# Turning the softmaxed tiles of nine attention pairs with VectorE and DRAM instead of TensorE

## The chip, the cores and the metric

The kernel runs on one core of a Trainium2 chip. The metric is the device time of one execution in microseconds (us); before the change it is 1721.01 us, the median of three runs that lie between 1719.12 and 1723.49 us. The core has a matrix engine (TensorE, PE), a vector engine (VectorE, DVE), a scalar engine (ScalarE, ACT), a general engine (GpSimd, POOL) and a queue engine that only issues transfers (SyncE, SP). Each of them works through its own list of instructions in order and waits for the others by semaphores. ACT and POOL issue transfers too, in the same list as their computation.

## The reference, cut to what matters

One layer of a hybrid backbone on 512 latent tokens of width 1024 (and 256 context tokens) is computed: a modulated norm, one input projection, three mixers side by side, an output projection, and an expert feed-forward part. The change lies in the third mixer, a neighbourhood attention with eight heads of width 64. The tokens are a grid of 8 rows by 64 columns; each query sees a window of 16 columns in all rows, and all 256 context tokens:

```python
s_loc = jnp.einsum('bqhd,bkwhd->bhqkw', q_row, k_blk).astype(jnp.float32) + bias[None]
s_ctx = jnp.einsum('bqhd,bchd->bhqc', q_row, k_ctx).astype(jnp.float32)
s_all = jnp.concatenate([s_loc.reshape(b, h, GRID_W, kh * GRID_W), s_ctx], axis=-1)
p = jax.nn.softmax(s_all, axis=-1).astype(v.dtype)
p_loc = p[..., :kh * GRID_W].reshape(b, h, GRID_W, kh, GRID_W)
return (jnp.einsum('bhqkw,bkwhd->bqhd', p_loc, v_blk)
        + jnp.einsum('bhqc,bchd->bqhd', p[..., kh * GRID_W:], v_ctx))
```

The product of `p` and the values sums over keys, so TensorE needs `p` with keys on the partitions, while the softmax leaves it with queries on the partitions. Each tile of `p` therefore has to be transposed between the two.

## The kernel before, in words

The queries are cut into four groups of 128 (16 columns in all 8 rows). With eight heads this makes 32 units, and two heads that lie together in one tile make a pair: 16 pairs, called 0 to 15 here. A unit has one tile of 128 queries by 512 keys (256 of the window's rows, 256 of the context). The work on it goes through small functions:

- `a_scores(m)` (L1166): eight matmuls of PE write the scores of both heads of pair m into two tiles `sps` in PSUM. There are only two such tiles, so the scores of the next pair wait until the exponentials of this pair have read them.
- `a_min(n)` (L1175, L1176): DVE takes the minimum over a row and adds the bias `nb`.
- `a_exp(n)` (L1183): ACT's exponential, from PSUM into the tile `pr`.
- `a_norm(n)` (L1188, L1189): DVE's reciprocal of the row sum; then the scaling of `pr`, by DVE for the pair's first head and by POOL for its second.
- `a_T(n)` (L1196): four PE transposes of 128 by 128 into PSUM; `a_copy(n)` (L1201): ACT's copy into the SBUF tile `pT`.
- `a_values(m)` (L1214): sixteen matmuls of PE into the PSUM tile `po`; `a_out(m)` (L210, L213): ACT rounds `po` to the high part `mBh`, DVE subtracts for the low part `mBl`.

Around this stands the output projection. A table of steps (`plan`, filled by `at(step, function, arguments)`) sets the order on all engines by hand. Pair m owns four steps from `a0 = A0 + 4 * m`. In these steps PE also works on 20 groups of six matmuls of the output projection (`o_part`, L220 to L222), one to two a pair; ACT and DVE convert the weights they need (`i_high` and `i_low`: `wh` at L210 and `wl` at L213, 128 by 1024); SP loads weights into four buffers `wraw` (L241), ACT loads the bias tiles `nb` (L1106). The values of pair m - 2 are computed with the scores of pair m. After the last pair, PE goes on with the rest of the output projection, and some of it is already drawn in between the last pairs.

Of the kernel before, what the change touches and what calls it, by code (L numbers as in the profile page):

```python
# [7 lines left out]
F32 = mybir.dt.float32  # L8
# [4 lines left out]
AF = mybir.ActivationFunctionType  # L13
# [4 lines left out]
P = 128  # L18
# [7 lines left out]
NH = 16  # L26
# [131 lines left out]
def build(tc, A, out, dbg=None):  # L158
    nc = tc.nc
    V, S, G, PE = nc.vector, nc.scalar, nc.gpsimd, nc.tensor  # L160
# [131 lines left out]
    gs_d = tc.dram_tile([P, NU], F32, name="gs_d")  # L292
    rs_d = tc.dram_tile([P, NU], F32, name="rs_d")
    mod_d = tc.dram_tile([2, 4, 512], F32, name="mod_d")
    cs_d = tc.dram_tile([2, NX * NH, P], F32, name="cs_d")

    def rstd_of(pool, ssq, n, width):
# [60 lines left out]
    for t in range(NT):  # L358
        src = A["x"][t * P:(t + 1) * P, :] if t < NX else A["ctx"][(t - NX) * P:(t - NX + 1) * P, :]
# [61 lines left out]
    def a_copy(e):  # L421
        am[e] = a1.tile([P, 256], F32, name="mod0", bufs=2)
        S.activation(am[e], aps[:, e % 2 * 256:e % 2 * 256 + 256], AF.Copy)
# [68 lines left out]
    for t in range(1, NT):  # L492
# [7 lines left out]
        if t < 4:  # L500
            x_copy(t - 1, 1)
    x_copy(3, 1, True)
    a_copy(0)
    w_split(0)
    x_copy(4, 1, True)
# [5 lines left out]
    for step in START:  # L511
        {"u": u_high, "l": u_low, "w": w_split, "v": w_low, "f": a_mod, "c": a_copy, "x": x_copy, "g": g, "a": a_mm, "gh": gh, "gl": gl}[step[0]](*step[1:])
# [150 lines left out]
    for cb in range(12):  # L663
# [5 lines left out]
        n = SEQ  # L669
        if cb < 10:  # L670
            S.activation(xp[:, 515:771], pc[:, :CTX], AF.Copy)
            n = 770
# [10 lines left out]
        dst = xsn[:, :, cb * P:(cb + 1) * P] if cb < 8 else Bn[:, :, (cb - 8) * P:(cb - 7) * P]  # L683
# [120 lines left out]
    def at(step, f, *a):  # L804
        plan.setdefault(step, []).append((f, a))
# [249 lines left out]
    for c in range(4):  # L1055
        b = U0 + UP * c
# [11 lines left out]
    for c in range(4):  # L1068
        b = O1 + OP * c
# [30 lines left out]
    au, pos_ = {}, {}  # L1100
# [48 lines left out]
    nat = natp.sb("na3", bufs=4)  # L1149
# [42 lines left out]
    def a_T(n):  # L1192
# [3 lines left out]
            PE.transpose(pt[:, j, :], pr[:, j * P:(j + 1) * P], ident)  # L1196
        au[n] = pt

    def a_copy(n):
        pT = nat.tile([P, 4, P], F32, name="pT")  # L1200
        S.activation(pT, au[n], AF.Copy)  # L1201
        au[n] = pT

    def a_values(m):

        hp, g, _ = units[2 * m]
        vl = vls[g]
        po = pos_[0] = psP.tile([P, P], F32, name="po")
        pTs = [au.pop(2 * m + hh) for hh in range(2)]
        for j in range(4):  # L1210
            for hh in range(2):
                h = hp * 2 + hh
                vv = vl[:, j, h * 64:(h + 1) * 64] if j < 2 else vc[:, j - 2, h * 64:(h + 1) * 64]
                PE.matmul(po[64 * hh:64 * hh + 64, :], vv, pTs[hh][:, j, :], start=j == 0, stop=j == 3)  # L1214

    def a_out(n):
        hp, g, _ = units[2 * n]
# [3 lines left out]
    for m in range(16):  # L1221
        a0 = A0 + 4 * m
        for hh in range(2):
            at(a0 + 2 + 2 * hh, a_load, 2 * m + 4 + hh)
        if m < 4:
            at(a0, v_load, m)
        at(a0, a_scores, m)
        if m:
            at(a0, a_T, 2 * m - 2)
            at(a0, a_copy, 2 * m - 2)  # L1230
        if m > 1:
            at(a0, a_values, m - 2)
            at(a0 + 1, a_out, m - 2)
        for hh in range(2):
            at(a0 + hh, a_min, 2 * m + hh)
            at(a0 + hh + 1, a_exp, 2 * m + hh)
            at(a0 + hh + 2, a_norm, 2 * m + hh)
        if m:
            at(a0 + 2, a_T, 2 * m - 1)
            at(a0 + 2, a_copy, 2 * m - 1)  # L1240
    a0 = A0 + 64
    at(a0, a_T, 30)
    at(a0, a_copy, 30)
    at(a0, a_values, 14)
    at(a0 + 1, a_out, 14)
    at(a0 + 2, a_T, 31)
    at(a0 + 2, a_copy, 31)
    at(a0 + 5, a_values, 15)
    at(a0 + 6, a_out, 15)


    wop = Pools()
# [3 lines left out]
    h = o1.tile([P, NX, D], F32, name="h")  # L1256
# [965 lines left out]
```

## Time and profile before

| | |
|---|---|
| median of three runs | 1721.01 us (1719.12 to 1723.49) |
| the profiled execution | 1722.26 us, span 1720.5 us |
| PE busy | 1698.8 us (99% of the span) |
| DVE busy | 1406.3 us (82%) |
| ACT busy | 839.4 us (49%) |
| POOL busy | 385.8 us (22%) |
| granted TensorE clock | 0.997 of full speed over the span |
| first scores of pair 0 | 361.14 us after the span's start |
| last values of pair 15 | 455.2 us after the span's start |

The time of the profiled execution is 1.76 us longer than the span, which begins with the first recorded instruction and ends with the last. Busy matmuls are pipelined, and a matmul that stands in the queue behind another counts as busy while it waits for its operand, so 99% is not the share in which PE computes. Attention takes some 95 us of 1720. How the engines share a stretch of the span is read from a view that sums busy time between two moments; what an engine waited for is read from the list of instructions in order of time, where the time in brackets is the idle time before the instruction and the name behind the arrow what ended it.

### The profile page before, as it was taken

Reading aid. Unit: us, or ns where it says so; the run is one execution under the profiler, and the core shown is the slowest. Engines: PE = TensorE matmul, PEld = TensorE weight load, DVE = VectorE, ACT = ScalarE, POOL = GpSimd, SP = SyncE. Lnnn points to the kernel's source line nnn. Section 1 sums busy time; section 2 is a strip of 40 time slices with the busy share of each in tenths; the row PEclk is TensorE's granted clock in tenths of the full one; section 3 lists DMA queues with packets and bytes.
Section 4 is the critical chain, followed back from the end, with each engine's and each line's share of the span. In section 5 each row is a group of like instructions: output and inputs, shape, how many; then the busy total and the mean of one; then the engine's idle time right before and its main releaser. Section 6 shows DMA issues by size and latency. Waiting matters only on the chain.

```text
span 1720.5 us, 26491 instructions
## 1 busy us (share of the span) xinstructions
PE 1698.8 (99%) x9556; PEld 1473.3 (86%) x9556; DVE 1406.3 (82%) x2668; ACT 839.4 (49%) x1507; POOL 385.8 (22%) x307
## 2 busy tenths in 40 slices
PE   9999999999999999999999999999999999999997
PEld 7888776776789889999999998888888888888886
DVE  6689479976546699879989997998988989889886
ACT  5443355565534333656776774444444444444444
POOL 0003134012336444031212111212211212211200
PEclk9999999999999999999999999999999999999999
DMA  9457466485536334587999999999999999999972
GB/s 368 134 158 233 153 201 176 147 277 164 167 107 196 115 117 135 173 290 266 349 348 348 342 328 353 386 404 365 392 364 380 368 418 382 385 366 381 383 275 106
DMA packets 200068, 473.08 MB, mean 275 GB/s; under 512 B 15080, under 2 KB 119112, under 8 KB 181984
## 3 DMA queue, kind: packets, MB, share of 16 engines
q1 hardware_dynamic: 151584, 268.41, 45.7%
q0 software_dynamic: 21136, 144.83, 22.0%
q10 hardware_dynamic: 27216, 58.14, 9.1%
q8 instruction: 75, 1.23, 0.3%
q14 instruction: 57, 0.47, 0.1%
HBM read 418.17 MB, written 55.26 MB: 275 GB/s over the span
## 4 chain that ended last, share of the span: by engine, by line
PE 82%; DVE 8%; DMA 3%; ACT 3%; issue 2%; ACTq 0%; SPq 0%; POOL 0%; DVEq 0%; POOLq 0%
PE pv L222 10%; PE pv L221 10%; PE pv L220 10%; PE pu L220 8%; PE pu L222 8%; PE pu L221 8%; PE acc L220 5%; PE acc L221 5%; PE acc L222 5%; DMA act_d<-act 3%; DVE wl L213 2%; PE acc L459 1%; PE acc L464 1%; PE acc L461 1%; PE sps L1166 1%
## 5 line engine op out<-in xcount | busy, mean ns | idle before, releaser
L210 ACT ACTIVATE wh<-wraw 128x1024 fp32r<-128x1024 f32 x328 | 342.0, 1053 | 219.3 <-PE acc L221 75.5
L213 DVE TENSOR_TENSOR wl<-wraw,wh 128x1024 fp32r<-128x1024 f32 x295 | 360.5, 1233 | 87.1 <-ACT wh L210 86.4
L220 PE MATMUL pu<-u2h,wh 128*128 128x368 f32 x1008 | 336.8, 334 | 1.5 <-ACT act L1516 1.3
L222 PE MATMUL pu<-u2h,wl 128*128 128x368 f32 x1008 | 332.3, 330 | 2.2 <-DVE wl L213 2.2
L221 PE MATMUL pu<-u2l,wh 128*128 128x368 f32 x1008 | 331.8, 329 | 0.0
L222 PE MATMUL pv<-wh,wwl 128*128 128x512 f32 x768 | 299.3, 390 | 0.0
L221 PE MATMUL pv<-wl,wwh 128*128 128x512 f32 x768 | 299.1, 389 | 0.0
L220 PE MATMUL pv<-wh,wwh 128*128 128x512 f32 x768 | 299.0, 389 | 0.1
L1795 POOL DMA_INDIRECT row<-in_peer_uv,idxG x128 | 158.3, 1236 | 615.7 <-DVE accG L1809 568.0
L222 PEld LDWEIGHTS pu<-u2h,wl 128*128 128x128 f32 x1008 | 189.6, 188 | 3.6 <-DVE wl L213 3.4
L220 PEld LDWEIGHTS pu<-u2h,wh 128*128 128x128 f32 x1008 | 189.7, 188 | 3.2 <-ACT act L1516 1.8
L221 PEld LDWEIGHTS pu<-u2l,wh 128*128 128x128 f32 x1008 | 189.8, 188 | 1.4
L210 ACT ACTIVATE wwh<-gd 128x384 fp32r<-128x384 f32 x124 | 65.1, 525 | 242.6 <-DVE gd L2040 229.8
L222 PEld LDWEIGHTS pv<-wh,wwl 128*128 128x128 f32 x768 | 144.2, 188 | 30.4 <-DVE wwl L213 0.3
L220 PEld LDWEIGHTS pv<-wh,wwh 128*128 128x128 f32 x768 | 144.2, 188 | 29.3 <-ACT wwh L210 0.5
L221 PEld LDWEIGHTS pv<-wl,wwh 128*128 128x128 f32 x768 | 144.1, 188 | 29.1
L1809 DVE SCALAR_TENSOR_TENSOR accG<-row,wG,accG 128x1024 f32<-128x1024 f32 x127 | 162.4, 1279 | 1.6
L1800 DVE CUSTOM_DVE_ANT_0 row<-row,u2G 128x1024 f32<-128x1024 f32 x128 | 154.8, 1218 | 0.0
L1883 ACT ACTIVATE stg<-gdps 128x512 f32<-128x512 f32 x96 | 100.9, 1163 | 19.5 <-ACT act L1516 14.9
L213 POOL TENSOR_TENSOR wl<-wraw,wh 128x1024 fp32r<-128x1024 f32 x33 | 79.1, 2402 | 101.7 <-ACT wh L210 71.2
L1516 ACT ACTIVATE act<-pu 128x368 f32<-128x368 f32 x90 | 42.7, 475 | 105.6 <-PE pu L222 61.5
L213 DVE TENSOR_TENSOR wwl<-gd,wwh 128x384 fp32r<-128x384 f32 x124 | 69.0, 556 | 21.9 <-ACT wwh L210 21.9
(481 smaller groups left out, 3017.3 us busy)
## 6 DMA issues: line engine op xcount, KB each, us to landing
wraw<-in_peer_ut SPq DMA_DIRECT2D x128, 512.0 KB
wraw<-in_peer_uv SPq DMA_DIRECT2D x128, 512.0 KB
gd<-gd_d SPq DMA_DIRECT2D x15, 1536.0 KB
gd_d<-stg ACTq DMA_DIRECT2D x11, 2048.0 KB
wraw<-in_w_in SPq DMA_DIRECT2D x40, 512.0 KB
acl<-act_d SPq DMA_DIRECT2D x92, 184.0 KB
act_d<-act ACTq DMA_DIRECT2D x90, 184.0 KB
cs<-cs_d SPq DMA_DIRECT2D x32, 256.0 KB
```

Of the source, the lines that this page charges most:

```text
L210: S.activation(hi, full, AF.Copy)
L213: (eng or V).tensor_tensor(lo, full, hi.bitcast(F32), ALU.subtract)
L220: PE.matmul(ps, ah, bh, start=start, stop=False)
L221: PE.matmul(ps, ah, bl, start=False, stop=False)
L222: PE.matmul(ps, al, bh, start=False, stop=stop)
L459: PE.matmul(px, h[:, k, :], uh[:, k, :], start=s, stop=False)
L461: PE.matmul(px, h[:, k, :], ul[:, k, :], start=False, stop=False)
L1516: S.activation(act, pu[:, :TU], AF.Gelu)
L1795: G.indirect_dma_start(out=rows[k], out_offset=None, in_=A["peer_uv"], in_offset=bass.IndirectOffsetOnAxis(ap=idxG[:, k:k + 1], axis=0))
L1800: V.tensor_tensor_reduce(row[:, 0:D], row[:, 0:D], u2G, 1.0, 0.0, ALU.mult, ALU.add, actG[:, k:k + 1])
L1809: V.scalar_tensor_tensor(accG, row[:, D:2 * D], wG[:, k:k + 1], accG, ALU.mult, ALU.add)
L1883: S.activation(stg[:, :, t0:t0 + 4].rearrange("p a t -> p t a"), ps, AF.Copy, scale=1.0 if full else 1.0 / GSCALE)
```

## The change

The tiles of pairs 5 to 13 (`TURN`) are no longer transposed by PE. DVE's transpose turns the sixteen 32 by 32 squares of each 128 by 128 block in place (`a_turn`); the squares still stand at the wrong partitions. POOL then stores the two turned tiles of a pair, 512 KB, to DRAM (`a_put`), and SP loads them back in four transfers of 32 partitions each, which bring the squares to the partitions where they belong (`a_get`). The tile `pT` now holds both heads of a pair and has three buffers; the turned tile `tT` has two. The values of a turned pair are computed with the scores four pairs later instead of two (`a_values(m - 4)`), and read `pT` through a pattern of four runs of 32. Pairs 0 to 4, 14 and 15 go by PE as before. Behind pair 15 the values now follow in the order 12, 14, 13, 15.

```diff
+    pt_d = tc.dram_tile([NH, P, 8 * P], F32, name="pt_d")
...
+    pT, tT = {}, {}
+    TURN = range(5, 14)
+
     def a_copy(n):
-        pT = nat.tile([P, 4, P], F32, name="pT")
-        S.activation(pT, au[n], AF.Copy)
-        au[n] = pT
+        m, hh = divmod(n, 2)
+        if hh == 0:
+            pT[m] = nat.tile([P, 2, 4, P], F32, name="pT", bufs=3)
+        S.activation(pT[m][:, hh], au.pop(n), AF.Copy)
+
+    def a_turn(n):
+        m, hh = divmod(n, 2)
+        if hh == 0:
+            tT[m] = nat.tile([P, 4, 2, P], F32, name="tT", bufs=2)
+        V.transpose(tT[m][:, :, hh, :].rearrange("p b (k q) -> p b k q", q=32),
+                    au.pop(n).rearrange("p (k b x) -> p b k x", k=4, b=4))
+
+    def a_put(m):
+        nc.gpsimd.dma_start(pt_d[m], tT.pop(m).rearrange("p b h x -> p (b h x)"))
+
+    def a_get(m):
+        pT[m] = nat.tile([P, 2, 4, P], F32, name="pT", bufs=3)
+        dst = pT[m].rearrange("p h k q -> p (h k q)").rearrange("p (a x) -> p a x", a=4)
+        src = pt_d[m].rearrange("(a k) (b x) -> b k a x", a=4, b=4)
+        for b in range(4):
+            nc.sync.dma_start(dst[32 * b:32 * b + 32], src[b])
...
-        pTs = [au.pop(2 * m + hh) for hh in range(2)]
+        t = pT.pop(m)
+        if m in TURN:
+            t = t.rearrange("p h k q -> p (h k q)").rearrange("p (a h k q) -> p h k a q", a=4, h=2, k=4)
...
-                PE.matmul(po[64 * hh:64 * hh + 64, :], vv, pTs[hh][:, j, :], start=j == 0, stop=j == 3)
+                PE.matmul(po[64 * hh:64 * hh + 64, :], vv, t[:, hh, j], start=j == 0, stop=j == 3)
...
-        if m:
+        if m and m - 1 not in TURN:
             at(a0, a_T, 2 * m - 2)
             at(a0, a_copy, 2 * m - 2)
-        if m > 1:
+        if m > 1 and m - 2 not in TURN:
             at(a0, a_values, m - 2)
             at(a0 + 1, a_out, m - 2)
+        if m - 4 in TURN:
+            at(a0, a_values, m - 4)
+            at(a0 + 1, a_out, m - 4)
...
-        if m:
+        if m and m - 1 not in TURN:
             at(a0 + 2, a_T, 2 * m - 1)
             at(a0 + 2, a_copy, 2 * m - 1)
+        if m - 1 in TURN:
+            at(a0 - 1, a_turn, 2 * m - 2)
+            at(a0 + 1, a_turn, 2 * m - 1)
+            at(a0 + 2, a_put, m - 1)
+        if m - 2 in TURN:
+            at(a0 + 2, a_get, m - 2)
     a0 = A0 + 64
     at(a0, a_T, 30)
     at(a0, a_copy, 30)
-    at(a0, a_values, 14)
-    at(a0 + 1, a_out, 14)
+    at(a0 + 2, a_values, 14)
+    at(a0 + 3, a_out, 14)
     at(a0 + 2, a_T, 31)
     at(a0 + 2, a_copy, 31)
-    at(a0 + 5, a_values, 15)
-    at(a0 + 6, a_out, 15)
+    at(a0 - 1, a_values, 12)
+    at(a0, a_out, 12)
+    at(a0 + 5, a_values, 13)
+    at(a0 + 6, a_out, 13)
+    at(a0 + 7, a_values, 15)
+    at(a0 + 8, a_out, 15)
```

How the instructions stand on the engines is shown at three places. Lines in the changed kernel are one higher from `pt_d` on and up to 38 higher behind the new functions. First DVE's list around pair 10, before: the low part of an output, the second head's minimum (three rows), a weight's low part, the norm of pair 10, and the first head's minimum of pair 11.

```order
L213 TENSOR_TENSOR mBl<-po,mBh 128x8x16
L1175 TENSOR_REDUCE mn<-sps 128x1
L1176 ISA sps,mn<-sps,nb,mn 128x256
L1176 ISA mn 128x1
L213 TENSOR_TENSOR wl<-wraw,wh 128x1024
L1188 RECIPROCAL sm<-sm 128x1
L1189 TENSOR_SCALAR pr<-pr,sm 128x512
L1188 RECIPROCAL sm<-sm 128x1
L1175 TENSOR_REDUCE mn<-sps 128x1
```

The same place now:

```order
L213 TENSOR_TENSOR mBl<-po,mBh 128x8x16
L1176 TENSOR_REDUCE mn<-sps 128x1
L1177 ISA sps,mn<-sps,nb,mn 128x256
L1177 ISA mn 128x1
L1213 STREAM_TRANSPOSE tT<-pr 128x4x128
L213 TENSOR_TENSOR wl<-wraw,wh 128x1024
L1189 RECIPROCAL sm<-sm 128x1
L1190 TENSOR_SCALAR pr<-pr,sm 128x512
L1189 RECIPROCAL sm<-sm 128x1
L1213 STREAM_TRANSPOSE tT<-pr 128x4x128
```

Two transposes have come in: the second head of pair 9 behind the second minimum, and the first head of pair 10 ahead of the first minimum of pair 11. `mBl` is now that of pair 6 instead of pair 8.

Second PE's list from the scores of pair 9 to those of pair 10, before:

```order
L1166 MATMUL sps<-kT,qT_120 128x256 x4
L1196 MATMUL pt<-cst,pr 128x128 x4
L1214 MATMUL po<-pT,vl_3712 64x128 x4
L1214 MATMUL po<-pT,vc 64x128 x4
L1196 MATMUL pt<-cst,pr 128x128 x4
L220 MATMUL acc<-wh,mAh 128x512
L221 MATMUL acc<-wl,mAh 128x512
L222 MATMUL acc<-wh,mAl 128x512
L220 MATMUL acc<-wh,mAh 128x512
L221 MATMUL acc<-wl,mAh 128x512
L222 MATMUL acc<-wh,mAl 128x512
L1166 MATMUL sps<-kT,qT_120 128x256 x4
```

And now:

```order
L1167 MATMUL sps<-kT,qT_121 128x256 x4
L1238 MATMUL po<-pT,vl_3585 64x128 x4
L1238 MATMUL po<-pT,vc 64x128 x4
L220 MATMUL acc<-wh,mAh 128x512
L221 MATMUL acc<-wl,mAh 128x512
L222 MATMUL acc<-wh,mAl 128x512
L220 MATMUL acc<-wh,mAh 128x512
L221 MATMUL acc<-wl,mAh 128x512
L222 MATMUL acc<-wh,mAl 128x512
L1167 MATMUL sps<-kT,qT_121 128x256 x4
```

Both rows of four transposes have gone; the values (now those of pair 5) follow the scores at once. A row here stands for one instruction of the program, and the profile counts two matmuls for each row of `sps` and `po`.

Third SP's list, now (`wraw` is a weight's load, each `pT` a quarter of a pair):

```order
L241 DMA wraw<-in_w_out 128x2x512 x4
L1224 DMA pT<-pt_d 32x4x256 x12
L241 DMA wraw<-in_w_out 128x2x512
L1224 DMA pT<-pt_d 32x4x256 x24
L241 DMA wraw<-in_w_out 128x2x512 x6
```

The loads of pairs 5 to 7 and 8 to 13 have come in, with one weight load between them; the six weight loads of the last row stand behind the last load of pair 13.

## The prediction

> **What bounds the kernel now.** I read the page first (PE is busy for 99% of the span), then the engines' busy time over the stretches of the attention, then the chain of waits in one of its pairs, then that pair's instructions in order of time. The second stretch runs from the scores of pair 7 to those of pair 15, eight pairs whose tiles the change turns, wholly or in part:
>
> ```profile
> core 0: us, PE busy (x) PEld busy (x) DVE busy (x) ACT busy (x) POOL busy (x), PEclk, DMA share, GB/s
> 361.00:399.60 38.60, 37.92 (x251) 26.96 (x250) 28.66 (x77) 26.31 (x53) 9.39 (x6) 1.00 0.77 242
> 399.60:443.80 44.20, 43.84 (x317) 31.36 (x316) 25.61 (x84) 25.75 (x61) 12.50 (x8) 1.00 0.45 141
> 443.80:456.40 12.60, 12.37 (x95) 9.18 (x95) 7.27 (x17) 8.43 (x18) 3.12 (x2) 1.00 0.28 86
> ```
>
> PE fills it, and DVE idles for 44.2 - 25.6 = 18.6 us. The chain of waits gives PE's steps of pair 9, with start and length:
>
> ```profile
> 410.97 1.64 PE sps L1166 x8
> 412.61 0.59 PE pt L1196 x4
> 413.19 1.02 PE po L1214 x16
> 414.22 0.59 PE pt L1196 x4
> ```
>
> With six matmuls of the output projection behind them (1.4 us) that is a pair's 5.23 us. But the scores have a stall in them, and the order of time shows what sets it:
>
> ```profile
> 410.41 0.14 DVE L1176 DVE_READ_ACCUMULATOR2_ANT mn<- 128x1 f32 x1
> 410.41 0.16 DVE L1188 RECIPROCAL sm<-sm 128x1 f32<-128x1 f32 x1
> 410.62 0.48 DVE L1189 TENSOR_SCALAR pr<-pr,sm 128x512 f32<-128x512 f32 x1
> 410.65 0.69 ACT L1183 ACTIVATE pr<-sps,mn 128x512 f32<-128x512 f32 x1 [0.67 <-DVE sm L1188]
> 410.90 1.71 PE L1166 MATMUL sps<-kT,qT 64*128 64x256 f32 x8
> 411.46 0.16 DVE L1188 RECIPROCAL sm<-sm 128x1 f32<-128x1 f32 x1 [0.36 <-ACT pr L1183]
> 411.48 0.73 PEld L1166 LDWEIGHTS sps<-kT,qT 64*128 64x128 f32 x6 [0.29 <-ACT pr L1183]
> 412.23 0.42 DVE L1175 TENSOR_REDUCE mn<-sps 128x1 f32<-128x256 f32 x1 [0.61 <-PE sps L1166]
> 412.54 0.66 PE L1196 MATMUL pt<-cst,pr 128*128 128x128 f32 x4
> 413.10 0.14 DVE L1176 DVE_READ_ACCUMULATOR2_ANT mn<- 128x1 f32 x1
> 413.12 0.66 PE L1214 MATMUL po<-pT,vl 128*64 128x128 f32 x8
> 414.26 0.28 ACT L210 ACTIVATE mBh<-po 128x128 fp32r<-128x128 f32 x1 [0.38 <-PE po L1214]
> 414.44 0.68 ACT L1183 ACTIVATE pr<-sps,mn 128x512 f32<-128x512 f32 x1
> 414.57 0.29 DVE L213 TENSOR_TENSOR mBl<-po,mBh 128x128 fp32r<-128x128 f32 x1 [1.33 <-ACT mBh L210]
> 414.78 0.41 DVE L1175 TENSOR_REDUCE mn<-sps 128x1 f32<-128x256 f32 x1
> 415.64 0.14 DVE L1176 DVE_READ_ACCUMULATOR2_ANT mn<- 128x1 f32 x1
> 415.88 0.69 ACT L1183 ACTIVATE pr<-sps,mn 128x512 f32<-128x512 f32 x1 [0.67 <-DVE sm L1188]
> 416.13 1.71 PE L1166 MATMUL sps<-kT,qT 64*128 64x256 f32 x8
> ```
>
> The pace is a loop over three engines. The second exponential of pair 8 ends at E = 411.34. It frees the score tile: PE goes on at E + 0.14 and ends the scores at E + 1.20. Then come four transposes, and `po` starts at E + 1.78; 1.14 later ACT rounds it; DVE's `mBl` waits for that, the second minimum of pair 9 stands behind `mBl` in DVE's list, and its exponential ends at 416.57, E + 5.23. The transposes between scores and `po` are in this loop (0.59); those behind `po`, and a second group of the output projection where a pair has one, run beside it.
>
> **The change part by part.** Removed: 18 times four transposes of PE, by the chain's 0.59 us 10.6 us of PE, and ACT's 18 copies `pT`. Added: 18 transposes of 128x512 on DVE, nine stores issued by POOL, 36 loads issued by SP. Moved: two groups of values to behind pair 15.
>
> No row shows DVE's transpose. The nearest rows are operations on as many elements, and one on twice as many:
>
> ```profile
> L1048 DVE TENSOR_TENSOR xsn<-yd,colv 128x512 f32<-128x512 f32 x1 | 0.7, 691 | 1.1 <-PE yd L1042 1.1
> L1189 DVE TENSOR_SCALAR pr<-pr,sm 128x512 f32<-128x512 f32 x9 | 4.4, 486 | 0.4
> L213 DVE TENSOR_TENSOR wl<-wraw,wh 128x1024 fp32r<-128x1024 f32 x3 | 3.7, 1219 | 0.0
> ```
>
> I take 0.69 us. From below 0.49 bounds it; from above 1.22, if each element takes twice the time. [...]
>
> The loop with these prices: `po` starts at E + 1.20, ACT rounds it at E + 2.34, and the first exponential could follow at E + 2.52 (0.18 later, as before). DVE ends the second minimum 0.79 ahead of E (415.78 against 416.57). Then: transpose of the other pair's second head to E - 0.06, reciprocal and norm (0.69) to E + 0.63, reciprocal 0.2, transpose to E + 1.52, first minimum (1.01, with 0.04 ahead) to E + 2.57 where it now ends at E + 1.90. First exponential at E + 2.67, `mBl` at E + 2.65, second minimum from E + 2.86 to 3.87, second exponential from E + 3.97 to **E + 4.66**. So a plain pair takes 4.7 instead of 5.23, and DVE hardly idles in it: of 1.2 us that PE gives up a pair, 0.5 arrive.
>
> The other pairs: no values fall to pairs 7 and 8 (those of 3 and 4 stand in 5 and 6, that of 5 in 9). In pair 8 the second minimum follows the first: to 3.6, exponential to 4.4. In pair 7 a `wl` (1.22) stands between them: 5.6. The `wl` at the ends of pairs 10 and 13 delays the first minimum of 11 and 14 to E + 3.8, `mBl` to 4.0, second minimum to 5.0, exponential to 5.8. Second groups of the output projection (pairs 7 and 11) still fit: 1.2 + 1.02 + 2.8 = 5.0. Sum for pairs 7 to 14: 5.6 + 4.4 + 4 x 4.7 (pairs 9, 10, 12, 13) + 2 x 5.8 = 40.4 for 44.2 us; pair 6 gains a plain pair's 0.5. Together 4.3 us.
>
> Behind pair 15 the work is PE's:
>
> ```profile
> 444.88 1.13 PE L1166 MATMUL sps<-kT,qT 64*128 64x256 f32 x6
> 452.71 0.66 PE L1196 MATMUL pt<-cst,pr 128*128 128x128 f32 x4 [0.23 <-POOL pr L1189]
> 454.69 0.66 PE L1214 MATMUL po<-pT,vl 128*64 128x128 f32 x8
> ```
>
> From the last scores on PE waits once, for 0.23 us, and the tail now holds values 11 to 15 instead of 13 to 15: 2 x 1.02 = 2.05 us more. Sum: 4.3 - 2.05 = **2.2 us gained**. The profiled execution (1722.26, span 1720.5) would come to 1720.0; against the median of 1721.0 I predict **1718.8**. With a transpose of 0.49 only pairs 7, 8, 11 and 14 gain 0.4 each more and the rest next to nothing: 1717. With 1.22 the eight pairs lose 2 x 0.53 each, 8.5 together: 1727.3.
>
> The transfers cost nothing in this sum. What covers them, by the store's nearest rows (512 KB to DRAM, issued by ACT at 518.56, seen landed by POOL at 521.16; and POOL's own issue):
>
> ```profile
> 518.56 0.33 ACTq L1403 DMA_DIRECT2D h_d<-h  x1
> 521.16 2.94 POOL L1415 TENSOR_TENSOR u2G<-xn,bcr 128x1024 f32<-128x1024 f32 x1 [2.85 <-DMA h_d<-h]
> 517.06 0.74 POOL L1412 DMA_DIRECT2D xs_d<-xn  x1
> ```
>
> The store thus takes 2.6 + 0.74 - 0.33 = 3.0 us on an idle path. Its tile `tT` is written again two pairs on: from the end of one pair's second transpose to the start of the pair after next's first there lie a period and the norm, 4.66 + 0.85 = 5.5 us. The loads then take four issues (0.33 each) and some 2.6 us; store and loads are 7 us, and the values come two periods and 1.2 us after the transpose, 10.5 us. Behind the loads on SP stand the weights for the part after attention:
>
> ```profile
> 439.74 15.66 SPq L241 DMA_DIRECT2D wraw<-in_w_out  x4
> 454.80 1.06 ACT L210 ACTIVATE wh<-wraw 128x1024 fp32r<-128x1024 f32 x1 [0.56 <-PE acc L222]
> ```
>
> The first of these four goes out at 439.74 and would now wait until some 445, for the loads of pair 13; the last conversion of the stage, at 454.80, waits for PE and not for a load, so I count nothing for that.
>
> **The rivals.** *A: the store comes back late, and DVE stands (slower).* Decided by 5.5 us. For it speaks the traffic: 1.05 MB a pair in 4.7 us is 223 GB/s on top of the 141 of the second stretch, 364 together, and the most that a 6 us piece of this stage moved is
>
> ```profile
> 372.00:378.00 6.00, 6.00 (x43) 4.37 (x44) 4.25 (x13) 4.52 (x11) 1.56 (x1) 1.00 1.11 372
> ```
>
> With up to three 512 KB transfers sharing this path the store can need 7 us. A first-head transpose waiting 1.5 us for it holds the next pair's first minimum behind it, then the exponential, then PE's scores, and with it the values: seven waits (pairs 7 to 13) are 10.5 us, the time 1729. Against it: both ends of the margin grow with every wait, and much of the 141 GB/s is loads with time to spare. [...]
>
> *B: the transpose takes the upper bound (slower).* 1727.3, as worked out. For it only that no row shows the operation.
>
> *C: all of PE's saving arrives (faster).* 1721.0 - 10.6 = 1710.4. For it speaks PE's 43.84 of 44.20 us; against it that the stall inside the scores is not PE's work, and the loop above.
>
> **How the numbers follow.** My own forecast 0.54, A 0.20, B 0.10, C 0.16. A measurement of this kernel tells some 0.3% (5.2 us) from no change, so my forecast is "the same"; its own range is 1715 to 1723. Faster by over 0.3%: C and a little of mine, 0.19. Slower: nearly all of A and B, 0.28. Same: 0.53. The range of 8 in 10 cuts the far parts of A and C: 1712 to 1730.
>
> **What would show it.** Right: DVE's transpose rows near 0.69, DVE busy for some 37 us in the stretch from pair 7's scores to pair 15's and that stretch near 40 us, the stall in the scores before second exponentials at 0.7 to 2 us, and two more groups of `po` behind pair 15. Wrong: DVE's transposes waiting for a transfer (A), rows of 1 us and more (B), a stretch of 35 us (C), or PE's `po` waiting for the loads of `pT`.

## The result: 12 us slower

| | median (us) | runs from to | against before, 95% interval |
|---|---|---|---|
| before | 1719.12 | 1715.72 to 1723.49 | |
| after | 1731.33 | 1725.68 to 1737.55 | 1.0070 (1.0048 to 1.0093) |

The forecast was 1718.8 us, the range 1712 to 1730. The profiled execution of the changed kernel took 1732.59 us (span 1730.8).

The busy time by stretches, with the stretches of the prediction (us of PE, PEld, DVE, ACT, POOL with the number of instructions, then granted clock, transfer share, GB/s), of the kernel after:

```profile
361.00:399.60 38.60, 37.66 (x247) 26.57 (x248) 29.86 (x80) 26.64 (x54) 9.69 (x7) 1.00 0.76 242
399.60:443.80 44.20, 30.09 (x166) 20.72 (x164) 25.36 (x74) 11.95 (x30) 14.37 (x14) 0.85 0.86 268
443.80:456.40 12.60, 11.74 (x84) 7.71 (x82) 10.12 (x28) 5.83 (x13) 5.03 (x5) 1.00 0.63 206
```

The loss lies in the second stretch. PE was busy there for 43.84 of 44.20 us before and is now for 30.09; the transfer share went from 0.45 to 0.86 and the granted clock from 1.00 to 0.85. (The share is the time of all packets, summed, over that of 16 engines; it passes 1 in places, as the 1.11 of the prediction's row from 372.00 us.) The waits between 360 and 480 us (us in total, times, longest) say for what:

```profile
PE po L1238 <- DMA pT<-pt_d: 13.5, 3, 7.7
DVE tT L1213 <- DMA pt_d<-tT: 5.1, 3, 2.9
```

PE's values stand for the loads, and DVE's transposes for the stores that still read their tile. The chain of waits from 405 to 440 us (start, length) shows where the loads lose the time:

```profile
406.99 6.00 DMA g1r<-mod_d
412.99 0.02 issue
413.01 6.39 DMA pT<-pt_d
419.40 0.14 issue
419.54 1.98 PE po L1238 x16
...
425.32 8.48 DMA pT<-pt_d
433.81 0.02 issue
433.82 4.02 DMA pT<-pt_d
437.84 0.06 issue
437.90 1.98 PE po L1238 x16
```

One load of 128 KB takes 6.39 us, another 8.48; the prediction had some 2.6. The transfers from 394 to 472 us (number, size of one, median us to landing) give 7.2 us for the one store whose landing this view shows, where it had 3.0:

```profile
pt_d<-tT POOLq DMA_DIRECT2D x9, 512.0 KB, 7.2
```

The trace holds the others too: each of the 74 transfers issued from 394 to 472 us moves its semaphore sixteen times, and these records, counted in the order of issue, give every landing. The nine stores took 2.9 to 8.1 us (median 6.7), the 36 loads 2.3 to 10.0 (median 4.5). The two medians make 11.2 us, and the values come 10.5 us after the transpose by the prediction.

In the chain, `g1r`, 512 KB that have nothing to do with the pair, stands ahead of a load of `pT`. What SP, which issues these loads in order, waited for between 400 and 460 us:

```profile
SPq L1224 <- DMA pt_d<-tT: 22.4, 6, 6.2
SPq L1224 <- DMA pT<-pt_d: 7.3, 4, 2.3
SPq L241 <- DVE mn L1176: 7.2, 1, 7.2
SPq L241 <- DVE wl L213: 5.4, 1, 5.4
SPq L1224 <- PE po L1238: 1.3, 2, 0.9
SPq L1224 <- DMA g1r<-mod_d: 0.9, 1, 0.9
SPq L1224 <- DMA nb<-in_nabias: 0.7, 1, 0.7
```

The first row is the wait that the data ask for (a load waits for its store, 6.2 us at the longest), and the one for `po` is for a free tile. The rows for `pT`, `g1r` and `nb` are neither: in the trace all transfers of SP and ACT in these 78 us (44 and 21) signal the same eight semaphores, and an issue waits until the last transfer on its semaphore has landed, as in the chain: `g1r` lands at 412.99, the load on its semaphore goes out at 413.01. POOL's nine stores signal eight others. The two rows of L241 are weight loads that wait for DVE to set their tile free: one ahead of pair 5's loads, whose store landed only as that wait ended, and one (5.4 us) ahead of pair 8's loads.

PE's instructions, three groups of the same eight matmuls:

```profile
419.54 1.12 PE L1238 MATMUL po<-pT,vl 128*64 128x128 f32 x8 [3.91 <-DMA pT<-pt_d]
425.05 0.66 PE L1238 MATMUL po<-pT,vl 128*64 128x128 f32 x8
...
437.90 1.12 PE L1238 MATMUL po<-pT,vl 128*64 128x128 f32 x8 [7.71 <-DMA pT<-pt_d]
```

Behind stands of 3.91 and 7.71 us they take 1.12 us instead of 0.66.

### The profile page after: what moved, and what is told of

Same layout as the page of the kernel before. It is cut to its first block, busy times and chain, and to the rows that moved or that the text cites. A ratio compares the mean times of both kernels' runs of the same rounds, so it can differ in the third digit from the quotient of the medians.

```text
span 1730.8 us, 26401 instructions
## 1 busy us (share of the span) xinstructions
PE 1694.8 (98%) x9484; PEld 1468.4 (85%) x9484; DVE 1416.9 (82%) x2686; ACT 830.6 (48%) x1489; POOL 390.2 (23%) x316
## 3 DMA queue, kind: packets, MB, share of 16 engines
q0 software_dynamic: 22432, 149.55, 22.4%
## 4 chain that ended last, share of the span: by engine, by line
PE 81%; DVE 9%; DMA 5%; ACT 3%; issue 2%; ACTq 0%; SPq 0%; DVEq 0%
PE pv L222 10%; PE pv L221 10%; PE pv L220 10%; PE pu L220 7%; PE pu L222 7%; PE pu L221 7%; PE acc L220 5%; PE acc L222 5%; PE acc L221 5%; DMA act_d<-act 3%; DVE wl L213 2%; PE acc L460 1%; PE acc L465 1%; PE acc L462 1%; DMA pT<-pt_d 1%
```

## The experiments

The theory (C): at the pace that the change makes, the stores and loads of nine pairs together with the rest fill the transfers' path, so trips come back later than four pairs allow. Its rivals: DVE's transposes and the new order cost it themselves (D); the prefetch of `h` and `g1r` in the same stretch (L); POOL's way of issuing the store (S); the order of SP's list (Q); the reuse of the eight semaphores (E); a trip too long for its lead on any path (M). Each run was timed against the kernel before on the same chip, so across runs the ratios compare better than the medians.

| run | median (us) | against before, 95% interval | last `mBl` at (us) |
|---|---|---|---|
| no_trip | 1713.47 | 0.9961 (0.9941 to 0.9980) | 452.5 |
| late_h | 1728.29 | 1.0049 (1.0031 to 1.0068) | 469.3 |
| put_act | 1729.66 | 1.0047 (1.0028 to 1.0065) | 470.5 |
| late_h_put_act | 1728.94 | 1.0045 (1.0028 to 1.0062) | 465.2 |
| w_behind | 1727.95 | 1.0041 (1.0025 to 1.0056) | 471.3 |
| w_late | 1726.37 | 1.0040 (1.0025 to 1.0055) | 465.8 |
| lead5 | 1723.76 | 1.0026 (1.0013 to 1.0040) | 463.2 |
| alt | 1718.21 | 0.9993 (0.9980 to 1.0005) | 455.3 |
| one_get | 1730.19 | 1.0066 (1.0046 to 1.0086) | 467.1 |
| one_get_w | 1724.77 | 1.0043 (1.0026 to 1.0059) | 467.1 |
| one_get_w_late | 1726.05 | 1.0047 (1.0032 to 1.0062) | 465.5 |
| lean | 1722.02 | 1.0005 (0.9991 to 1.0018) | 463.4 |
| lean_tail | 1717.36 | 0.9981 (0.9967 to 0.9996) | 458.7 |
| w_tail | 1722.44 | 1.0010 (0.9998 to 1.0023) | 461.4 |
| alt6 | 1718.06 | 0.9985 (0.9972 to 0.9999) | 457.0 |

The last column is the start of the last `mBl` in the profiled execution, the end of the attention; it is 457.0 before and 472.8 after. It is no pure measure of the loss: PE does 27 matmuls of the output projection with `mBh` or `mBl` (0.23 us each) ahead of the last values in the changed kernel and in lean_tail, 15 in no_trip, one before.

### Without the trips

```diff
-            tT[m] = nat.tile([P, 4, 2, P], F32, name="tT", bufs=2)
+            tT[m] = pT[m] = nat.tile([P, 4, 2, P], F32, name="pT", bufs=5)
...
-            at(a0 + 2, a_put, m - 1)
-        if m - 2 in TURN:
-            at(a0 + 2, a_get, m - 2)
```

> Leaves out the nine stores and the 36 loads: the values of the nine pairs read the tile that DVE turned as it stands (five buffers of 4 KB instead of 3 + 2), so blocks of 32 are in the wrong places of the output; every instruction of PE, DVE and ACT and their order are those of the changed kernel. If the round trip through DRAM makes the loss (T): PE's values no longer stand for loads (13.5 us in the changed kernel, seen from 360 to 470), DVE's transposes no longer stand for stores (5.1), the stretch from pair 7's scores to pair 15's is about 40 us, and the time is that of the prediction's sum, 1719 (1715 to 1722). If DVE's transposes and the new order themselves cost what was lost (D): 1728 to 1733, and the stretch stays above 48 us.

Measured: 0.9961 of before, some 6.7 us less. T holds and D falls: the new work and the new order are a gain, larger than the prediction's, and the nine trips turn it into a loss; 1.0070 - 0.9961 is 18.7 us. PE's instructions, the second part of the scores of pairs 9, 10, 11, 12 and 13 (of pair 12 all eight matmuls in one row):

```profile
406.72 1.13 PE L1167 MATMUL sps<-kT,qT 64*128 64x256 f32 x6 [0.17 <-ACT pr L1184]
411.37 1.13 PE L1167 MATMUL sps<-kT,qT 64*128 64x256 f32 x6 [0.28 <-ACT pr L1184]
416.01 1.13 PE L1167 MATMUL sps<-kT,qT 64*128 64x256 f32 x6 [0.26 <-ACT pr L1184]
421.04 1.13 PE L1167 MATMUL sps<-kT,qT 64*128 64x256 f32 x8
425.69 1.13 PE L1167 MATMUL sps<-kT,qT 64*128 64x256 f32 x6 [0.28 <-ACT pr L1184]
```

Plain pairs follow each other after 4.65, 4.64 and 4.65 us, where the prediction's loop gave 4.66; the pair with a `wl` takes 5.03, where it gave 5.8. From the first scores of pair 7 (397.34) to those of pair 15 (434.18) there are 36.8 us against 40.4 foretold and 44.2 before. The transfer share of the second stretch, same view:

```profile
399.60:443.80 44.20, 42.25 (x279) 28.71 (x279) 37.39 (x107) 20.23 (x50) 14.82 (x10) 1.00 0.47 154
```

### Prefetch moved, stores on another queue

late_h (the edits of put_act stand below it; late_h_put_act has both):

```diff
-    at(O0 + 34, row_bc, g1r, 1, 0, nc.scalar)
+    at(O0 + 60, row_bc, g1r, 1, 0, nc.scalar)
-        at(O0 + 36 + 3 * t, nc.scalar.dma_start, h[:, t, :], ...)
+        at(O0 + 56 + t, nc.scalar.dma_start, h[:, t, :], ...)
```

```diff
-        nc.gpsimd.dma_start(pt_d[m], tT.pop(m)...)
+        nc.scalar.dma_start(pt_d[m], tT.pop(m)...)
```

> The four loads h of 512 KB and the one of g1r, issued by ACT at 407 to 427 us in the changed kernel, are issued some 20 to 30 us later (with pairs 14 and 15); they are needed at 473. Nothing else moves. If the round trip is late because it shares the transfers' path with these 2.5 MB (L): the stores land in 4 to 5 us instead of 7.2, PE's stand for pT falls from 13.5 us to under 4, and the time goes to 1719 to 1723. If POOL's way of issuing the store is what is slow (S), or the margin is too short in any traffic: the stores stay at 6 to 7 us, PE's stand stays over 9 us, the time 1728 to 1732.

> The nine stores are issued by ACT's queue, at the same step, instead of by POOL's; everything else as in the changed kernel. [...] If it is the traffic (L): the landing stays at 6 to 7 us and the time at 1729 to 1733.

> Both edits: h and g1r later, and the stores on ACT's queue. If the two causes add (L and S): no stand for pT, the time of the kernel without the trip, 1717 to 1720. If only one of them matters, no more than 1 us below the better of the two single edits.

Measured: 1.0049, 1.0047 and 1.0045; each takes some 4 us off the loss (the intervals overlap that of the change itself), and together they take no more. late_h lies where it should if the moved loads are not the cause by themselves; the time of put_act lies where L had it. As single causes, L and S both fall. In late_h PE still stood 9.8 us for `pT`, and the moved loads fill another place, the 6 us from 442:

```profile
442.00:448.00 6.00, 4.98 (x35) 3.43 (x35) 3.91 (x13) 3.10 (x8) 2.16 (x2) 1.00 1.02 406
```

In put_act the stores did land sooner, as they should by S: 2.9 to 5.8 us, median 3.6, for 6.7 in the changed kernel. But the stands only changed place. Its waits between 360 and 480 us:

```profile
ACT mBh L210 <- DMA nb<-in_nabias: 11.8, 2, 8.9
PE po L1238 <- DMA pT<-pt_d: 8.6, 2, 5.4
ACT wh L210 <- DMA pT<-pt_d: 3.7, 1, 3.7
```

The 8.9 us of the first row are not clearly a wait for `nb`: PE's `po` behind its stand of 5.4 us ended at 437.64, and ACT went on at 437.68. The third row is ACT standing at the issue of an `nb` load whose semaphore a `pT` load held; ACT's list now has the stores too. Of the 3.1 us by which the stores' landing shortened, the issue itself is some 0.26 (0.59 us on POOL in the changed kernel, 0.33 on ACT in put_act, both medians); where the rest comes from was not shown. It is not what the loss hangs on: with the quicker landing put_act still stands at 1.0047, and at 1.0045 with late_h's edit beside it; and in lean_tail below POOL issues the same nine stores, and their median is 4.0.

### SP's order, half the trips, a longer lead

```diff
# w_behind; w_late is this and late_h
         ilows.pop(0)()
-        i_load(i + 4)
+        if i == 10:
+            at(O0 + 43, i_load, 14)
+        else:
+            i_load(i + 4)
# alt (the tail's a_values for pair 12 goes too)
-    TURN = range(5, 14)
+    TURN = (5, 7, 9, 11, 13)
# lead5 (the tail then holds 11 and 12 in place of 12 and 13)
-    TURN = range(5, 14)
+    TURN = range(5, 13)
-        if m - 4 in TURN:
-            at(a0, a_values, m - 4)
-            at(a0 + 1, a_out, m - 4)
+        if m - 5 in TURN:
+            at(a0, a_values, m - 5)
+            at(a0 + 1, a_out, m - 5)
```

> The one weight load (item 14, 512 KB) that stands in SP's queue ahead of pair 8's four loads is issued right behind them (step 43 for 41). In the changed kernel SP stood 5.4 us at it, until DVE's wl at 425.3 set its tile free, and the loads of pair 8 and 9, whose stores had landed long before, with it. If the order of SP's queue is a main part of the loss (Q): the stand of PE at the values of pair 8 (7.7 us, and with it the half clock behind it) goes to under 3, the time to 1722 to 1726. If the path is simply full (C: store and loads are 1.05 MB a pair): PE stands elsewhere as long, 1729 to 1732.

> The same edit and the later h and g1r of the second run. Q and a small part from the traffic (the run alone gave 1728.3): 1717 to 1722, PE's stands for pT under 3 us in all. C: 1727 to 1729, as with the later h alone.

> Only the pairs 5, 7, 9, 11 and 13 are turned; 6, 8, 10 and 12 keep PE's transposes and their values two pairs behind, so that each pair from 9 to 15 has one value group and one more than before stands in the tail. Half the traffic of the trip, and twice the time between two stores. If the path's load or its few tiles are what is late (C): no stand over 1 us, and something like half of what the kernel without trip gains: 1715 to 1718. If the length of one trip against four pairs of lead is what is late whatever the load (M), or SP's queue (Q): stands of some us at the values of pairs 7 to 9 remain, 1720 to 1726.

> Values five pairs behind the scores instead of four, pairs 5 to 12 turned (13 by PE), as many value groups in the tail as in the changed kernel. Stores and loads are issued at the same steps. If it is the length of the trip (M, or Q's stand of 5 us at one place): 4.7 us more for each trip take PE's 13.5 us of stand to under 3, time 1718 to 1723. If the path is full (C): the pairs go on only as fast as their transfers, DVE's stand for stores (5.1) grows in place of PE's, 1726 to 1731.

In lead5 two value groups stand at the same step of pair 15, and the second one's result is written for both, so one group is missing in its output; the work on every engine is as described.

w_behind: 1728.0, 2 us above Q's band and 1 under C's. The stand at pair 8's values went, and the one at those of pair 6 grew from 3.91 to 7.24 us, as C has it (PE's instructions):

```profile
422.36 1.12 PE L1241 MATMUL po<-pT,vl 128*64 128x128 f32 x8 [7.24 <-DMA pT<-pt_d]
```

Q could not give back the whole 5.4 us: in the changed kernel the store of pair 8 landed at 422.4, 2.9 us before its loads went out, and that of pair 9 was only issued at 423.93, so the two had not landed "long before", as the expectation has it.

w_late: 1726.4, near C's band of 1727 to 1729. alt: 1718.2, just above C's 1715 to 1718, and nearly without stands. Its second stretch, and PE's wait for loads between 360 and 480 us:

```profile
399.60:443.80 44.20, 42.46 (x295) 29.57 (x295) 32.27 (x97) 22.19 (x55) 16.23 (x13) 1.00 0.83 253
```

```profile
PE po L1238 <- DMA pT<-pt_d: 0.5, 1, 0.5
```

PE is busy for 42.46 us at full clock. So half the trips fit, with the same lead and the same prefetch in the stretch, and weight loads on SP between the pairs' loads as before. Its stores landed after 3.1 to 5.5 us (median 3.3), its loads after 2.9 to 7.0 (4.6): 7.9 us by the medians, inside the 10.5. The share gives the number for C: 0.83 with five trips and 0.47 with none, so 0.072 a trip; nine trips at that pace would need 0.47 + 0.65 = 1.12 of the path, an estimate.

lead5: 1723.8, between the bands of both theories. PE's stand for `pT` fell from 13.5 to 1.2 us (as M says), DVE's for the stores grew from 5.1 to 6.8 (as C says), and the share was the highest of all:

```profile
399.60:443.80 44.20, 37.56 (x211) 25.47 (x210) 31.69 (x93) 16.25 (x40) 17.07 (x16) 0.88 0.97 304
```

Its stores were as late as in the changed kernel (median 7.0 us). It doesn't tell M from C by itself, and it has one trip fewer.

### One load for a pair

```diff
-        nc.gpsimd.dma_start(pt_d[m], tT.pop(m).rearrange("p b h x -> p (b h x)"))
+        t = tT.pop(m).rearrange("p b h x -> p (b h x)")
+        dst = pt_d[m].rearrange("(b k) (a x) -> a k b x", a=4, b=4)
+        for a in range(4):
+            nc.gpsimd.dma_start(dst[a], t[32 * a:32 * a + 32])
-        for b in range(4):
-            nc.sync.dma_start(dst[32 * b:32 * b + 32], src[b])
+        nc.sync.dma_start(pT[m].rearrange("p h k q -> p (h k q)"), pt_d[m])
```

> The tile in DRAM is laid out so that a pair comes back in one load of 512 KB (4 KB a partition) instead of four of 128 KB; POOL writes it in four stores of 128 KB instead of one, and so issues 27 more (0.6 us each, 2.4 a pair). Bytes, lead, order as in the changed kernel. All transfers of SP and ACT share eight semaphores, and an issue waits until the last transfer on its own has landed: in the changed kernel the loads of one pair went out over several us, SP standing for g1r, nb and other pairs' pT between them. If that reuse is a main part of the loss (E): SP no longer stands for nb, h, g1r or pT, PE's stand for pT falls from 13.5 to under 6 us, time 1722 to 1727. If the path is full (C): stands and time as in the changed kernel, 1729 to 1733.

> The same, and the weight load of item 14 behind pair 8's load, as in the run w_behind (1728.0 by itself). E and Q add: 1718 to 1723. C: 1727 to 1730.

> The same, and h and g1r later, as in late_h. If the three causes (semaphores E, SP's order Q, the prefetch in the same stretch L) are the loss together: PE's and DVE's stands for the trip under 3 us in all, and the time near the kernel without the trip, 1714 to 1718: below both kernels. C: 1726 or more, as the run w_late (1726.4).

Measured: 1730.2, 1724.8 and 1726.1. The first and the third are in C's bands, the second is between the two. What SP waited for in one_get between 400 and 460 us:

```profile
SPq L1224 <- DMA pt_d<-tT: 37.9, 12, 7.3
SPq L241 <- DVE mn L1176: 7.5, 1, 7.5
SPq L241 <- DVE wl L213: 4.5, 1, 4.5
SPq L241 <- DVE sm L1189: 3.9, 2, 2.7
SPq L1224 <- PE po L1238: 0.3, 1, 0.3
```

The waits for `g1r`, `nb` and `pT` are gone, and the time stays; PE still stands 7.6 us for `pT` and DVE 8.8 for stores. That SP's wait for the stores grew from 22.4 to 37.9 us shows no more than that SP comes to them earlier. By the landings a pair's store takes 7.0 us (median, from the first of its four issues to the last landing) and its load 5.5, together again over 10.5. So E falls as a main part: the semaphores were a place where the lateness showed, not its source. The test is not quite clean: four issues make the store longer by themselves, 4.9 us for the first pair's, where it is 3.1 in the changed kernel. (The profiled execution of one_get is its fastest, 1722.96 us; in the median the loss is larger than this view shows.)

### The path made empty

In lean, on top of w_late:

```diff
+            if n > 16:
+                au[n] = au["nbK"]
+                return
-            au[n] = nbp.tile([P, 256], F32, name="nb")
+            au[n] = nbp.tile([P, 256], F32, **(dict(name="nbK", bufs=1) if n == 16 else dict(name="nb")))
+            if n == 16:
+                au["nbK"] = au[n]
```

lean_tail is lean, and w_tail is w_behind, with `g1r` and `h` at steps O0 + 66 and O0 + 66 + t. alt6 is alt with `TURN = (3, 5, 7, 9, 11, 13)`.

> The run w_late (h and g1r later, one weight load behind pair 8's loads), and the bias tiles nb of pairs 8 to 15 are left out: 15 loads of 128 KB fewer, those pairs add the tile of their first head instead of their own, so the probabilities are others. The nine trips through DRAM, their order, waits and lead stay. The stretch of 44.2 us from pair 7's to pair 15's scores had a transfer share of 0.47 in the kernel without trips and 0.83 in the one with five pairs turned; nine would need 0.47 + 0.36 x 9 / 5 = 1.12 at that pace, less some 0.18 without h and g1r and some 0.1 without nb: 0.8 to 0.85. If the path's load is what makes the trips late (C): PE's stands for pT under 3 us, DVE's for stores under 2, the time 1714 to 1719. If the trip is too long for its lead on a path with room too (M): PE and DVE stand for some 10 us in all, as in w_late, and the time is 1724 to 1727.

> As the run lean (15 bias tiles nb left out, one weight load behind pair 8's loads), with h and g1r issued by ACT behind the last trip (about 455 us) instead of with pairs 14 and 15. In lean the pairs ran at the pace of the kernel without trips, and what was left stood at 437 to 449 us, where h and g1r met the loads of pairs 11 and 12 (1.3 and 3.4 us, and half clock behind). If the path's load is the cause (C): these two stands go under 1 us, the time 1714 to 1718. If the trip is too long for its lead in any case (M): the stands at pairs 11 and 12 remain, 1720 to 1723.

> The same with all bias tiles loaded, so the output is whole: the changed kernel with h and g1r behind the last trip and the one weight load behind pair 8's loads. C: share needed some 0.94 at the pace without trips, so short stands remain: 1719 to 1723, against 1726.4 of w_late. M: 1724 to 1727.

> As the run alt, with pair 3 turned as well (3, 5, 7, 9, 11, 13); nothing else. Each turned pair took 1.0 us off in the kernel without trips (9.1 us before the tail for nine), and the tail keeps one value group more than before. C: the stretch before pair 7 has a share of 0.75 and gets 0.08 more, no stands: 1716 to 1718, a little under alt's 1718.2. If pair 3's loads are held behind weight loads in SP's queue, which stands for DVE there (7 us at 395): 1718 to 1721.

lean: 1722.0, in no band. Until 437 us it ran at the pace of no_trip with all nine trips in it; then PE's values stood for the loads of pairs 11 and 12, where `h` and `g1r` now fell. PE's instructions, and the 6 us from 436:

```profile
440.53 0.66 PE L1246 MATMUL po<-pT,vl 128*64 128x128 f32 x8 [1.34 <-DMA pT<-pt_d]
...
449.56 1.12 PE L1246 MATMUL po<-pT,vl 128*64 128x128 f32 x8 [3.37 <-DMA pT<-pt_d]
```

```profile
436.00:442.00 6.00, 4.24 (x31) 2.71 (x32) 3.20 (x9) 2.36 (x6) 2.16 (x2) 1.00 1.03 391
```

lean_tail takes them away from there and settles C against M: 1717.4, as C said (1714 to 1718). Even in its slowest execution, which is the one profiled (1721.94 us), the waits for trips between 360 and 480 us are these two:

```profile
DVE tT L1221 <- DMA pt_d<-tT: 0.9, 1, 0.9
PE po L1246 <- DMA pT<-pt_d: 0.3, 1, 0.3
```

The second stretch in lean_tail:

```profile
399.60:443.80 44.20, 41.98 (x266) 28.28 (x267) 37.86 (x110) 20.36 (x50) 19.46 (x18) 1.00 0.70 235
```

The median time to landing of its stores and of its loads, from 394 to 472 us:

```profile
pt_d<-tT POOLq DMA_DIRECT2D x9, 512.0 KB, 4.0
pT<-pt_d SPq DMA_DIRECT2D x36, 128.0 KB, 3.5
```

The stores lie between 3.1 and 4.8 us. The view has four of the 36 loads; all of them, from the semaphore records, lie between 2.3 and 5.1, median 2.9. Nine trips with four pairs of lead make stands of 1.2 us in all where the path has a share of 0.70. M falls. By the ratios lean_tail is still some 3.4 us behind no_trip (0.9981 and 0.9961, with intervals that overlap); more than these stands was not traced. w_tail, with the bias tiles and so a whole output, gave 1722.4 (C: 1719 to 1723, M: 1724 to 1727), with stands of 2.7 us of PE and 2.2 of DVE. alt6 gave 0.9985 (0.9972 to 0.9999), 1718.1, on the edge of its two bands (1716 to 1718, 1718 to 1721), with 0.5 us of PE's stands for loads. It is the whole kernel that comes out best; that it is faster than before by some 0.15% the interval barely supports, and it is less than a measurement of this kernel was said to tell.

Left open: lean_tail and w_tail have also fewer transfers on the eight semaphores (in lean_tail SP stands for none of `g1r`, `nb` and `pT`) and the weight load behind pair 8's loads. one_get shows that the reuse alone isn't the source and w_behind that SP's order alone isn't; how much each adds once the path is full was not separated. What neither can touch is the time from a store's issue to its landing, since POOL issues it on semaphores of its own: a median of 6.7 us in the changed kernel, 4.0 in lean_tail, 3.3 in alt.

## Why the prediction was wrong, point by point

- **The step that failed is "The transfers cost nothing in this sum".** They cost 18.7 us (1.0070 - 0.9961 of 1719). Mis-sized was the trip: a store 3.0 us, a load 2.6, with the issues 7 us together against 10.5. Both durations came from one row, 2.6 us long, and were used for a stretch that the change itself fills; nor was that an idle path, as the prediction has it, but one with a share of 0.77 in these 2.6 us. As prices of one transfer alone they hold: the first store of the changed kernel landed after 3.1 us, the quickest load after 2.3. Measured in its fullest part, from 404 to 430 us, the stores took 6.7 to 8.1 us, and the chain shows loads of 6.39 and 8.48. In lean_tail, with room on the path, the medians are 4.0 and 2.9, within the margin.
- **The number that should have sounded it** stood in the prediction, under rival A: 223 GB/s of trips and 141 of the rest are 364, against 372 as the most that a 6 us piece of this stage had moved. It was used to price one rival and not held against the forecast's own pace; as a share of the path it comes to 1.12.
- **Rival A (0.20) named the mechanism**, but only half the place, and its number (1729 for 1731) is in part luck: it puts 10.5 us on a loop of 1718.8, and the runs show 18.7 on one of 1713.5. DVE did stand for stores (5.1 us for 10.5 foretold), while PE's stand for the loads, 13.5 us, was no term of it and stood only in the last sentence on what would show the forecast wrong. The half clock behind the stands was in neither.
- **Weight loads on SP** were looked at in one direction. Those behind the loads cost nothing, as said; at the one ahead of pair 8's loads SP stood 5.4 us, which was not seen, since SP reaches it early and waits there for DVE's `wl`. It held these loads 2.9 us beyond the landing of their store.
- **DVE's transpose** was right: 0.69 foretold, and after

```profile
L1213 DVE STREAM_TRANSPOSE tT<-pr x18: 692/708/712, 395.5 to 451.5; 128x512 f32<-128x512 f32 x18
```

  (least, median and greatest ns of the transposes in the kernel after). The 0.69 was the author's estimate, from the row of 691 ns for as many elements between those of 486 and 1219; no run had shown the operation. Rival B (1.22 us) is out.
- **The loop** was right where it could be seen alone: 4.65 us for 4.66 in plain pairs of no_trip. Its exceptions were too dear: pairs 7 to 14 took 36.8 us and not 40.4, most of it in pairs 8 (3.2 for 4.4) and 14 (4.8 for 5.8). So the gain without trips was 6.7 us and not 2.2. Rival C's 10.6 us did not arrive even there.
- **The range** ended at 1730, one us short of the median.

## What to carry to other kernels

Price a new transfer twice: its time on the path as it is, and the share of the path that all transfers need together at the pace the change is to reach. Here that sum was 1.12, and lead, queue and issuer each took back only a part (4 to 8 us of 18.7, the most with a longer lead and one trip fewer), while half the trips left next to no stand. In these runs the stands for trips are 0.5 and 1.2 us at measured shares of 0.83 (alt) and 0.70 (lean_tail), and 18.6 at 0.86 in the changed kernel, so here the measured share did not tell how late the kernel was; the share needed at the planned pace, 1.12, would have. An issue list that runs in order needs its entries ahead of the new ones checked as well as those behind.

## What the runs showed of the hardware that was not expected

Stands of PE cost more than their length in the changed kernel. The granted clock of the second stretch is 0.85, and the eight matmuls of `po` take 1.12 us behind stands of 3.91 and 7.71 us, 0.66 elsewhere. The two pieces of the stretch at half clock (same view as the stretches):

```profile
419.43:422.84 3.41, 3.30 (x19) 2.77 (x20) 0.95 (x3) 0.95 (x3) 0.00 (x0) 0.50 0.92 269
433.08:443.32 10.24, 5.42 (x26) 4.00 (x28) 3.01 (x9) 1.73 (x5) 0.98 (x2) 0.50 0.71 216
```

PE was busy for 3.30 + 5.42 = 8.72 us of them, so some 4.4 us of its time there went to the clock, an estimate (half of 8.72). By the time of the same eight matmuls, half clock followed the stands of 3.91 and 7.71 us here, 7.24 in w_behind and 3.37 in lean (1.12 us each), and none the stands of 1.85 us here and 1.34 in lean (0.66 each). In no_trip, alt and lean_tail, where PE's stands for trips are under 0.6 us, the clock of the stretch is 1.00.
